# Feed-forward activations stored as two fp32r halves, with the loads, rows and norms of the down stages rearranged

## The chip, the cores and the metric

The kernel runs on one core of a Trainium2 chip. The metric is the device time of one execution in microseconds (us). The version before has a median of 2328.14 us over three runs (2327.58 to 2334.51). TensorE is called PE below, VectorE DVE, ScalarE ACT, GpSimd POOL, and the queue of SyncE, which issues nearly all transfers, SP.

## The reference, cut to what matters

Two layers run over 1024 tokens of width 1024. Each layer has a mixer and a feed-forward part, both inside sandwich RMSNorm (pre-norm, sub-layer, post-norm, residual add):

```python
def sandwich(x, g_pre, g_post, fn):
    return x + rmsnorm(fn(rmsnorm(x, g_pre)), g_post)

def swiglu(h, w_gate, w_up, w_down):
    return (jax.nn.silu(h @ w_gate) * (h @ w_up)) @ w_down
```

The change sits in the two `swiglu` parts. Their inner width is 2816, which is 22 blocks of 128.

## The kernel before, in words

**Split arithmetic.** A product of float32 matrices is made of three matmuls in fp32r: an operand `a` is kept as a high half `hi` (a rounding to fp32r) and a low half `a - hi`, and the products high-high, high-low and low-high are added (`mm3`, line 114; `hi`/`lo` are written `wh`/`wl` for weights, `hh`/`hl` for h). `wsplit` (line 1118) makes the halves of a weight tile: an ACT cast for `wh` (line 1121), a POOL subtraction for `wl` (line 1123).

**Up stage** (`Ffn.up`, line 1218; `pair`, line 1168). For 11 pairs of blocks, Strassen-like sums of weights and inputs give seven products per pair instead of eight, 24 matmuls each. From these come four quarters of h per pair (SiLU on ACT, line 1144, and a product on DVE, line 1145) and three sums of quarters on POOL (`store`, line 1178). All seven tiles of 128 x 512 go to DRAM as plain float32 (`h_s`, blocks 0 to 6, lines 1147 and 1179). In layer 0 the preparation of the state-space layer (`s5_prep`, line 578) runs as a generator beside the pairs: one step at each `emit` and each `store`. Its tiles tagged `pbig` have six buffers.

**Down stage** (`Ffn.down`, line 1229). For each group of two pairs, seven products with sums of `w_down` blocks accumulate into two SBUF tiles `out`. `hx` (line 1249) loads a block of h (512 KB for two pairs, four buffers, on SP) and splits it again: ACT makes `hh` (line 1252), DVE makes `hl` (line 1253). `drain` (line 1262) adds PSUM to `out`, mostly on DVE (line 1271). After the last `top`, the rows of the first half of `out` go through `end` while the last two products of the second half run; then the second half follows.

**Row norms** (`sandwich`, line 157). Per 128 tokens: the residual row is loaded into `r` (line 162), ACT sums the squares (line 106), POOL makes the reciprocal root (lines 97 and 98), DVE scales by it and by the post-norm gain (line 165) and adds the residual (line 166), the row is stored (line 170), and in layer 0 a second sum of squares and a second scaling (line 173) follow for the next layer. In layer 1 the two scalings are lines 168 and 169. In layer 0 the rows are then transposed on PE (`to_T`, line 175) as input of `mla_in` (line 807).

**Order.** The framework orders the instructions of each engine ahead of time by a simulated timeline; each engine, and SP, then runs its own list strictly in order. A load whose buffer is not free holds all that stand behind it in SP's list. The gains of the post-norm (`gpost`, `gpre`, line 111) and the rows `r` are loaded as early as that order places them, which is at the start of the down stage.

Of the kernel before, what the change touches and what calls it, by code (L numbers as in the profile page):

```python
# [10 lines left out]
F32 = mybir.dt.float32  # L11
# [24 lines left out]
class Trunk:  # L36
# [64 lines left out]
    def sumsq(self, a):  # L101
        ss = self.small.tile([P, 1], F32, tag="ss", name="ss")
        junk = self.tmp.tile([P, D], BF16, tag="t", name="junk")
        if len(a.shape) == 3:
            junk = junk.rearrange("p (k c) -> p k c", k=2)
# [3 lines left out]
    def bcast(self, pool, ap, name):  # L109
        t = pool.tile([P, D], F32, tag=name, name=name, bufs=1)  # L110
        self.nc.sync.dma_start(t, ap.partition_broadcast(P))
        return t
# [44 lines left out]
    def sandwich(self, acc, tb, res, hout, gpost, gpre, r, eng, m=None):  # L157
# [420 lines left out]
    def s5_prep(self, pool):  # L578
# [7 lines left out]
        big = lambda n: pool.tile([P, 2, 9 * 16], F32, tag="pbig", name=n, bufs=6)  # L586
# [58 lines left out]
        tb = sm("tb", (P, 8, 16))  # L645
# [18 lines left out]
        for ch in range(2):  # L664
# [28 lines left out]
            de = sm("de", (32, 4, 16))  # L693
# [360 lines left out]
class Ffn:  # L1054
    def __init__(self, K, p, left, right):
        self.K, self.nc, self.left, self.right = K, K.nc, left, right
        self.gu, self.dn = K.io[p + "gu"], K.io[p + "dn"]
        self.h_s = K.dr.tile([7, NF // 2, P, HALF], F32, name=p + "h_s")
# [82 lines left out]
    def emit(self, g, u, blk, i):  # L1141
# [4 lines left out]
        if blk is not None:  # L1146
            nc.sync.dma_start(self.h_s[blk, i], g)

    def pre(self, i, step):
# [8 lines left out]
        else:  # L1158
# [5 lines left out]
            self.emit(c[0], c[1], 0, i)  # L1164
# [3 lines left out]
    def pair(self, i):  # L1168
# [32 lines left out]
        self.emit(c12[:, 0], c12[:, 1], None, i)  # L1201
        store(c11[1], c11[0], c12[:, 0], ALU.subtract, 6)
# [330 lines left out]
```

## Time and profile before

| What | us |
|---|---|
| median of three runs | 2328.14 |
| the profiled execution | 2332.52 |
| its span | 2330.1 |
| mean granted TensorE clock of it | 0.968 |
| up stage of layer 0 / down stage of layer 0 (from the span's start) | about 538 to 961 / 961 to 1197 |
| up stage of layer 1 / down stage of layer 1 | about 1676 to 2081 / 2081 to 2330 |

The profiled execution is 4.4 us above the median of the runs, and 2.4 us of it lie outside the span. Times in the rows are counted from the span's start. PE's busy time is modelled, since matmuls overlap, so its waits say more than its busy share.

### The profile page before, as it was taken

The numbers are of one execution on the slowest core, as the hardware profiler recorded it, in microseconds if no ns is written. First come the engines' busy times: TensorE is split into PE (matmuls) and PEld (weight loads), VectorE is DVE, ScalarE is ACT, GpSimd is POOL, SyncE is SP. The second block draws the span as 40 slices with busy tenths as digits, with TensorE's granted clock in tenths as the row PEclk, the third lists the DMA queues.
The fourth block names the chain that finished last, engine by engine and source line by source line (L and its number), as shares of the span: only waits on it lengthen the run. The fifth ranks groups of instructions, "written<-read, shape, count | busy, mean of one in ns | idle before, by whom it ended". The sixth has DMA issues, their size and how long they took to land.

```text
span 2330.1 us, 27167 instructions
## 1 busy us (share of the span) xinstructions
PE 2157.9 (93%) x9684; PEld 1746.3 (75%) x9684; DVE 1594.9 (68%) x2175; ACT 945.2 (41%) x1413; POOL 1265.7 (54%) x740
## 2 busy tenths in 40 slices
PE   7999889898999999899969888999899999989987
PEld 5887677676788878687758767876688888878866
DVE  6859567689856865477884578656964444447788
ACT  5554555453222332333344346654532322234332
POOL 4997202134665556776644455421575656577674
PEclk9999999899999999899979999999999999999999
DMA  5234683243332343644542674324332323255354
GB/s 204 71 109 140 167 206 112 76 168 107 107 117 100 123 136 104 221 140 134 173 160 80 193 232 141 113 97 160 119 131 72 133 73 131 73 178 185 112 167 149
DMA packets 150662, 315.32 MB, mean 135 GB/s; under 512 B 20224, under 2 KB 43904, under 8 KB 150528
## 3 DMA queue, kind: packets, MB, share of 16 engines
q1 hardware_dynamic: 150528, 313.60, 41.4%
q8 instruction: 76, 1.25, 0.2%
q14 instruction: 58, 0.48, 0.1%
HBM read 214.39 MB, written 96.01 MB: 133 GB/s over the span
## 4 chain that ended last, share of the span: by engine, by line
PE 68%; DVE 16%; DMA 6%; issue 4%; ACT 3%; POOL 3%; SPq 0%; POOLq 0%; DVEq 0%; ACTq 0%
PE b L115 29%; PE psd L115 13%; PE psw L115 6%; PE psc L115 5%; PE psq L115 3%; PE po L115 2%; DVE hl L1253 2%; DVE acc L1271 2%; PE pss L1038 2%; PE trp L365 1%; POOL wl L1123 1%; DVE wt L1042 1%; PE pss L452 1%; DMA bm<-k_s 1%; PE psv L115 1%
## 5 line engine op out<-in xcount | busy, mean ns | idle before, releaser
L1123 POOL TENSOR_TENSOR wl<-raw,wh 128x1024 fp32r<-128x1024 f32 (+1 forms) x238 | 614.1, 2588 | 412.3 <-ACT wh L1121 399.7
L115 PE MATMUL b<-T,wh 128*128 128x512 f32 x1408 | 438.4, 392 | 2.2 <-DVE F L1172 2.2
L1121 ACT CAST wh<-raw 128x1024 fp32r<-128x1024 f32 (+1 forms) x238 | 241.9, 1023 | 433.0 <-PE b L115 251.7
L115 PE MATMUL b<-B,wh 128*128 128x512 f32 x1056 | 337.4, 400 | 15.0 <-DVE c L1163 10.5
L115 PEld LDWEIGHTS b<-T,wh 128*128 128x128 f32 x1408 | 263.8, 188 | 62.3 <-issue 2.8
L115 PE MATMUL b<-T,wl 128*128 128x512 f32 x704 | 276.4, 393 | 1.6 <-POOL wl L1123 1.6
L115 PE MATMUL psd<-wh,hh 128*128 128x512 f32 x616 | 240.6, 400 | 32.6 <-ACT hh L1252 18.9
L115 PEld LDWEIGHTS b<-B,wh 128*128 128x128 f32 x1056 | 203.0, 193 | 62.5 <-ACT B L1089 7.3
L115 PE MATMUL psd<-wl,hh 128*128 128x512 f32 x616 | 241.4, 396 | 0.0
L115 PE MATMUL psd<-wh,hl 128*128 128x512 f32 x616 | 235.2, 396 | 1.3 <-DVE hl L1253 1.3
L1271 DVE TENSOR_TENSOR acc<-acc,psd 128x512 f32<-128x512 f32 (+1 forms) x208 | 177.8, 884 | 60.1 <-PE psd L115 60.0
L115 PE MATMUL b<-B,wl 128*128 128x512 f32 x528 | 210.9, 400 | 3.6 <-POOL wl L1123 3.6
L115 PE MATMUL psw<-wh,jt 128*128 128x512 f32 x512 | 176.0, 410 | 16.0 <-ACT jt L488 9.3
L1172 DVE TENSOR_TENSOR p<-p,b 128x1024 f32<-128x1024 f32 (+1 forms) x88 | 83.5, 950 | 135.3 <-PE b L115 134.9
L1252 ACT CAST hh<-hr 128x1024 fp32r<-128x1024 f32 (+1 forms) x84 | 82.2, 979 | 223.8 <-PE psd L115 206.6
L115 PEld LDWEIGHTS psd<-wh,hh 128*128 128x128 f32 x616 | 117.2, 190 | 67.3 <-ACT hh L1252 23.9
L1253 DVE TENSOR_TENSOR hl<-hr,hh 128x1024 fp32r<-128x1024 f32 (+1 forms) x84 | 152.5, 1826 | 16.6 <-ACT hh L1252 16.6
L115 PEld LDWEIGHTS b<-T,wl 128*128 128x128 f32 x704 | 132.1, 188 | 32.7 <-POOL wl L1123 2.8
L91 POOL TENSOR_TENSOR wl<-raw,wh 128x1024 fp32r<-128x1024 f32 x48 | 122.2, 2558 | 58.4 <-ACT wh L89 58.4
L115 PEld LDWEIGHTS psd<-wh,hl 128*128 128x128 f32 x616 | 117.1, 190 | 28.9 <-DVE hl L1253 2.6
L115 PEld LDWEIGHTS psd<-wl,hh 128*128 128x128 f32 x616 | 117.5, 191 | 25.5
L1173 DVE TENSOR_TENSOR raw<-raw 128x1024 f32<-128x1024 f32 x66 | 106.7, 1617 | 41.3 <-POOL wl L1123 40.2
(386 smaller groups left out, 4314.4 us busy)
## 6 DMA issues: line engine op xcount, KB each, us to landing
raw<-in_l_gu_dram SPq DMA_DIRECT2D x96, 512.0 KB, 3.6
hr<-l_h_s SPq DMA_DIRECT2D x70, 512.0 KB, 4.1
raw<-in_l_dn_dram SPq DMA_DIRECT2D x48, 512.0 KB, 3.8
l_h_s<-F SPq DMA_DIRECT2D x66, 256.0 KB, 2.3
raw<-in_w_in_dram SPq DMA_DIRECT2D x27, 512.0 KB, 3.5
l_h_s<-c SPq DMA_DIRECT2D x44, 256.0 KB, 2.1
l_h_s<-p SPq DMA_DIRECT2D x44, 256.0 KB, 2.6
raw<-in_l_w_out_dram SPq DMA_DIRECT2D x16, 512.0 KB, 4.2
```

The costliest lines, as they stand in the source:

```text
L91: nc.gpsimd.tensor_tensor(lo, raw, hi.bitcast(F32), op=ALU.subtract)
L115: mm = lambda *t, **k: self.nc.tensor.matmul(*t, skip_group_check=go, **k)
L365: nc.tensor.transpose(tr[:, jj * P:(jj + 1) * P], Wt[:, offs[jj] + i * P:offs[jj] + (i + 1) * P], self.ident)
L452: nc.tensor.matmul(ps[:, b0:b0 + bw], Q[c][v][:, j * P:(j + 1) * P], M[c][:, b0:b0 + bw], start=v == 0, stop=v == 1)
L1038: nc.tensor.matmul(ps[:, ks], a[:, js], b[:, ks], start=first, stop=last)
L1121: nc.scalar.copy(hi[:, 0:n], r[:, 0:n])
L1123: nc.gpsimd.tensor_tensor(lo[:, 0:n], r[:, 0:n], hi[:, 0:n].bitcast(F32), op=ALU.subtract)
L1172: add = lambda o, a, b: v.tensor_tensor(o, a, b, op=ALU.add)
L1173: sub = lambda o, a, b: v.tensor_tensor(o, a, b, op=ALU.subtract)
L1252: nc.scalar.copy(hi[:, 0:n], r[:, 0:n])
L1253: v.tensor_tensor(lo[:, 0:n], r[:, 0:n], hi[:, 0:n].bitcast(F32), op=ALU.subtract)
L1271: v.tensor_tensor(dst, dst, ps, op=ALU.add)
```

## The change

1. **Halves in DRAM.** `h_s` gets a further dimension of two. A new method `put` makes the halves in the up stage: ACT copies the tile into `hs` (fp32r, two buffers), SP stores that, the low half is subtracted in place, on POOL for the blocks 6, 1, 5 and 4 (the sums that POOL itself made) and on DVE for 3, 0 and 2, and SP stores it too. `hx` then loads both halves (1 MB for two pairs, four buffers) and splits nothing.
2. **First loads.** The loads of the blocks 0, 5, 1 and 4 of the first group are issued by ACT.
3. **Late rows and gains.** The gains and the first four residual rows get a small ACT copy from `out` first, so that their loads cannot start before the last but one `top` has been added up. The eight rows are loaded there and passed to `end`.
4. **Staggered norms.** `sandwich` becomes a generator `sand` with pauses; `skew` runs the rows of one half shifted by one stage against each other. All four rows of the first half go before the last two products. In layer 0 the second half's sums of squares wait for the last transposed piece of the first half.
5. **Room.** `pbig` in `s5_prep` has three buffers instead of six, and three small tiles move into other tags. In layer 1 the two extra buffers of the split weights are closed during the up stage (`K.less()`, `K.more(right)`), so `wh` and `wl` have three buffers there instead of five.

```diff
-        self.h_s = K.dr.tile([7, NF // 2, P, HALF], F32, name=p + "h_s")
+        self.h_s = K.dr.tile([7, NF // 2, P, 2, HALF], F32, name=p + "h_s")
...
+    def put(self, blk, i, g):
+        nc = self.nc
+        hi = self.hs.tile([P, HALF], F32R, tag="hs", name="hs", bufs=2)
+        nc.scalar.copy(hi, g)
+        nc.sync.dma_start(self.h_s[blk, i, :, 0], hi.bitcast(F32))
+        eng = nc.gpsimd if blk in (6, 1, 5, 4) else nc.vector
+        eng.tensor_tensor(g.bitcast(F32R), g, hi.bitcast(F32), op=ALU.subtract)
+        nc.sync.dma_start(self.h_s[blk, i, :, 1], g)
...
-        both(u4, 3)
-        store(c12[:, 1], c12[:, 0], u4[:, 0], ALU.add, 1)
-        store(u4[:, 1], c12[:, 1], c11[0], ALU.subtract, 5)
+        both(u4)
+        pool(c12[:, 1], c12[:, 0], u4[:, 0], ALU.add)
+        self.put(3, i, u4[:, 0])
+        pool(u4[:, 1], c12[:, 1], c11[0], ALU.subtract)
+        self.put(0, i, c11[0])
+        self.put(1, i, c12[:, 1])
...
-        both(p1, 2)
-        store(p1[:, 1], p1[:, 0], u4[:, 1], ALU.subtract, 4)
+        both(p1)
+        pool(p1[:, 1], p1[:, 0], u4[:, 1], ALU.subtract)
+        self.put(5, i, u4[:, 1])
+        self.put(2, i, p1[:, 0])
+        self.put(4, i, p1[:, 1])
...
-        def hx(blk, i, n):
-            r = hraw(blk, i, n)
-            hi, lo = half("hh"), half("hl")
-            nc.scalar.copy(hi[:, 0:n], r[:, 0:n])
-            v.tensor_tensor(lo[:, 0:n], r[:, 0:n], hi[:, 0:n].bitcast(F32), op=ALU.subtract)
-            return hi, lo
+        def hx(blk, i, n):
+            r = hp.tile([P, 2, 2, HALF], F32R, tag="h", name="h", bufs=4)
+            queue = nc.scalar if i == 0 and blk in (0, 5, 1, 4) else nc.sync
+            queue.dma_start(r[:, 0:n].bitcast(F32), self.h_s[blk, i:i + n].rearrange("g p s c -> p g s c"))
+            return r
...
         top(i1, n)
+        late = out[0][:, 0, 0, 0:1]
+        gains(late)
+        rows = []
+        for tb in range(8):
+            r = ap.tile([P, D], F32, tag="r", name="r", bufs=4)
+            if tb < 4:
+                nc.scalar.copy(r[:, 0:1], late)
+            nc.sync.dma_start(r, res[tb * P:(tb + 1) * P, :])
+            rows.append(r)
         B = top(i2, n)
...
-        end(0, out[0], rows(2), 0)
+        end(0, out[0], rows[0:4], 0)
...
-        end(0, out[0], rows(2), 2)
...
+    def skew(self, rows):
+        live = []
+        for g in [*rows, None, None]:
+            for x in [g] * (g is not None) + live[::-1]:
+                next(x, None)
+            live.append(g if g is not None else iter(()))
...
-        big = lambda n: pool.tile([P, 2, 9 * 16], F32, tag="pbig", name=n, bufs=6)
+        big = lambda n: pool.tile([P, 2, 9 * 16], F32, tag="pbig", name=n, bufs=3)
...
+    K.less()
     G.up()
+    K.more(right)
```

## Rows read from the trace of the kernel before

**Rows 1.** The page: the chain that ended last, by engine.
```profile
PE 68%; DVE 16%; DMA 6%; issue 4%; ACT 3%; POOL 3%; SPq 0%; POOLq 0%; DVEq 0%; ACTq 0%
```

**Rows 2.** Busy time by stretch: start:end, us, engines (instructions), clock, DMA share, GB/s.
```profile
975.00:1100.00 125.00, 125.00 (x540) 102.12 (x539) 90.35 (x86) 46.67 (x54) 81.84 (x35) 0.99 0.45 148
...
1680.00:2080.00 400.00, 400.00 (x1739) 326.70 (x1739) 197.29 (x201) 113.07 (x125) 244.08 (x117) 1.00 0.30 102
```

**Rows 3.** PE's first down matmul of layer 0 in the timeline, idle time before it.
```profile
972.51 0.80 PE L115 MATMUL psd<-wh,hh 128*128 128x512 f32 x1 [11.61 <-ACT hh L1252]
```

**Rows 4.** The chain of waits, 905 to 985 us: start, us, what.
```profile
956.36 6.06 DMA gpost<-in_l_ffn_post_dram
...
962.44 8.95 DMA hr<-l_h_s
...
972.51 12.69 PE psd L115 x43
```

**Rows 5.** Transfers: up stage of layer 1, then 975 to 1100 us; us to landing.
```profile
l_h_s<-F SPq DMA_DIRECT2D x30, 256.0 KB, 2.5
...
hr<-l_h_s SPq DMA_DIRECT2D x18, 512.0 KB, 3.8
```

**Rows 6.** Who waited for whom on PE, 2079 to 2092 us: us, times, longest.
```profile
PE psd L115 <- ACT hh L1252: 5.4, 1, 5.4
PE psd L115 <- DVE hl L1253: 1.3, 1, 1.3
```

**Rows 7.** Busy time by stretch around the ends of the up and down stages.
```profile
964.30:978.00 13.70, 5.49 (x13) 4.02 (x14) 5.30 (x4) 5.22 (x5) 9.01 (x5) 0.50 1.04 405
2083.80:2094.00 10.20, 6.29 (x14) 4.51 (x15) 7.59 (x3) 3.14 (x3) 8.08 (x4) 0.50 0.92 333
...
1196.00:1210.00 14.00, 1.29 (x9) 0.93 (x8) 9.41 (x9) 6.13 (x11) 7.86 (x10) 0.63 0.55 181
1210.00:1222.00 12.00, 6.56 (x25) 4.51 (x23) 10.53 (x11) 5.19 (x10) 3.48 (x5) 0.50 0.50 172
```

**Rows 8.** Who waited for whom on PE, 1100 to 1197 us, then 2215 to 2319 us.
```profile
PE psd L115 <- DVE acc L1271: 4.2, 6, 1.5
...
PE psd L115 <- DVE acc L1271: 9.3, 7, 2.4
```

**Rows 9.** A group on DVE, 1100 to 1200 us: busy, mean ns, idle before.
```profile
L1253 DVE TENSOR_TENSOR hl<-hr,hh 128x1024 fp32r<-128x1024 f32 x14 | 26.6, 1900 | 0.0
```

**Rows 10.** Timeline of DVE: the first scaling of three rows.
```profile
1177.66 1.29 DVE L165 SCALAR_TENSOR_TENSOR acc<-acc,rstd,gpost 128x1024 f32<-128x1024 f32 x1 [1.00 <-ACT hh L1252]
...
1188.15 3.41 DVE L165 SCALAR_TENSOR_TENSOR acc<-acc,rstd,gpost 128x1024 f32<-128x1024 f32 x1 [0.72 <-ACT wh L89]
...
1199.24 3.36 DVE L165 SCALAR_TENSOR_TENSOR acc<-acc,rstd,gpost 128x1024 f32<-128x1024 f32 x1
```

**Rows 11.** Timeline of SP in the up stage of layer 0.
```profile
815.86 11.31 SPq L699 DMA_DIRECT2D T_s<-K  x16
...
942.19 14.08 SPq L1115 DMA_DIRECT2D raw<-in_l_dn_dram  x3
```

**Rows 12.** The chain of waits, 2290 to 2331 us: the last row.
```profile
2325.09 1.28 DVE r L169
```

**Rows 13.** Groups on POOL, ACT and DVE in layer 1's up stage, 1680 to 2080 us.
```profile
L1123 POOL TENSOR_TENSOR wl<-raw,wh 128x1024 fp32r<-128x1024 f32 x72 | 181.3, 2519 | 142.7 <-ACT wh L1121 133.3 <-DMA raw<-in_l_gu_dram 9.3
L1178 POOL TENSOR_TENSOR F<-F 128x512 f32<-128x512 f32 x11 | 14.3, 1297 | 13.6 <-DVE F L1145 13.6
...
L1121 ACT CAST wh<-raw 128x1024 fp32r<-128x1024 f32 x72 | 75.7, 1052 | 212.2 <-PE b L115 143.2 <-DVE raw L1173 51.2 <-POOL wl L1123 9.1
L1144 ACT ACTIVATE F<-F 128x512 f32<-128x512 f32 x22 | 13.9, 632 | 51.5 <-DVE F L1172 51.5
...
L1145 DVE TENSOR_TENSOR F<-F 128x512 f32<-128x512 f32 x22 | 17.2, 783 | 2.0
```

**Rows 14.** Who waited for whom on PE, 538 to 960 us.
```profile
PE b L115 <- POOL wl L1123: 5.2, 4, 3.5
```

More of the change, by code (lines that the diff above doesn't have):

```diff
@@ L99, in rstd, with sumsq @@
         return r
-    def sumsq(self, a):
+    def sumsq(self, a, late=None):
         ss = self.small.tile([P, 1], F32, tag="ss", name="ss")
         junk = self.tmp.tile([P, D], BF16, tag="t", name="junk")
+        if late is not None:
+            self.nc.scalar.copy(junk[:, 0:1], late)
         if len(a.shape) == 3:
@@ L107, in sumsq, with bcast @@
         return self.rstd(ss, D, RMS_EPS)
-    def bcast(self, pool, ap, name):
+    def bcast(self, pool, ap, name, late=None):
         t = pool.tile([P, D], F32, tag=name, name=name, bufs=1)
+        if late is not None:
+            self.nc.scalar.copy(t[:, 0:1], late)
         self.nc.sync.dma_start(t, ap.partition_broadcast(P))
@@ L161, in sandwich @@
         acc, r = v3(acc), v3(r)
-        nc.sync.dma_start(r, v3(res[rows, :]))
-        rs = self.sumsq(acc)
+        if res is not None:
+            nc.sync.dma_start(r, v3(res[rows, :]))
+        rs = self.sumsq(acc, late)
         if m is None:
             nc.vector.scalar_tensor_tensor(acc, acc, rs, v3(gpost), op0=ALU.mult, op1=ALU.mult)
+            yield
             eng.tensor_tensor(r, r, acc, op=ALU.add)
@@ L172, in sandwich @@
             rs = self.sumsq(r)
+            yield
             nc.vector.scalar_tensor_tensor(acc, r, rs, v3(gpre), op0=ALU.mult, op1=ALU.mult)
@@ L1200, in pair @@
         c11 = self.c11.pop(i)
-        self.emit(c12[:, 0], c12[:, 1], None, i)
-        store(c11[1], c11[0], c12[:, 0], ALU.subtract, 6)
+        both(c12)
+        pool(c11[1], c11[0], c12[:, 0], ALU.subtract)
+        self.put(6, i, c11[1])
         sub(A21, A11, A21)
@@ L1227, in up, with down @@
         self.xs.close()
-    def down(self, end, ap):
+    def down(self, end, ap, gains, res):
         nc, K, v = self.nc, self.K, self.nc.vector
@@ L1235, in down @@
         seen = set()
-        half = lambda tag: hp.tile([P, 2, HALF], F32R, tag=tag, name=tag, bufs=4)
         def ld(blk, i, n):
@@ L1320, in down @@
         W4 = [w4(B, n, v)]
-        rows = lambda k: [ap.tile([P, D], F32, tag="r", name="r", bufs=4) for _ in range(k)]
-        end(0, out[0], rows(2), 0)
+        end(0, out[0], rows[0:4], 0)
         C12, C22 = ld(1, i1, n), ld(3, i1, n)
@@ L1334, in down @@
         hs.close()
-        end(1, out[1], rows(4), 0)
+        end(1, out[1], rows[4:8], 0)
 @with_exitstack
```

48 lines of the change are left out of this document (22 added, 26 removed).

## The prediction

> **What bounds the kernel now.** I read the chain that ended last first, by engine [rows 1]: two thirds of the span are PE, so the question in each stage is whether PE waits there at all. The table of stretches answers it [rows 2]: in the up stage of layer 1 and in the middle of the down stage of layer 0 PE is busy from end to end (1739 matmuls in 400 us, 0.230 us each, so 5.5 us per product of 24). Work taken off other engines there is worth nothing. PE waits at the edges of the down stages, in three kinds of places.
>
> *Starts.* In layer 0 PE stands still for 11.61 us before the first down matmul [rows 3]. The chain [rows 4] shows why: SP issues the gains at 956.36, the first h load only at 962.44, and the load takes 8.95 us, against a median of 3.8 in the middle of the stage [rows 5], because gains and four residual rows are in flight ahead of it. In layer 1 PE waits 5.4 and 1.3 us for the two halves of the first h [rows 6]. After both gaps the granted clock is 0.50 (the 1.2 GHz level): PE was busy 5.49 and 6.29 us in those stretches [rows 7], and at 2.4 GHz this would have taken half, so 2.7 and 3.1 us go with the gaps.
>
> *Last groups.* PE waits 4.2 us in layer 0 and 9.3 us in layer 1 for DVE to empty PSUM [rows 8]. DVE is late because the low halves of h stand in its list: 14 of 1.900 us, with no idle time before them [rows 9].
>
> *The change of layers.* The last down matmul of layer 0 ends near 1197 and the projections begin near 1222. In between PE is busy 1.29 and 6.56 us out of 26 [rows 7]. It waits for the row norms, which run one after another: the first scalings of three rows start at 1177.66, 1188.15 and 1199.24, 10.8 us apart [rows 10], although the wait-free scalings take 1.29 us and a row has three DVE passes, so about 3.9 us.
>
> **The change, part by part.** The sum is made against the profiled execution, 2332.5 us, which lies 4.4 above the median of the runs.
>
> *Start of layer 0.* The ACT queue does not hold behind SP's weight loads (three of which kept SP 14.08 us here [rows 11]), gains and rows come later, and no split follows the load. At stake: 11.6 + 2.7 = 14.3 us. I cannot see where ACT's list will put the load; if right behind the last SiLU, near 959, a load of twice 512 KB at 4 to 5 us (above the 3.8 of one [rows 5]) lands 3 to 4 us after PE is free. I take 10 saved; bounds 3 and 14.3.
>
> *Start of layer 1.* At stake 5.4 + 1.3 + 3.1 = 9.8 us. The split goes for certain, the load's own time may stay: 6 saved; bounds 2 and 9.8.
>
> *Last groups.* Without the 26.6 us of low halves DVE has room for the drains in the 100 us of that stretch. Of 4.2 and 9.3 us I take 4 and 8; bounds 0 and all.
>
> *The change of layers.* Staggered, the rows cost DVE some 3.9 us each instead of 10.8. Four rows are 16 us, and beside them run 22 us of matmuls (the last two products of two groups, 96 matmuls at 0.230), with eight drains. So the first half is normed about when PE finishes, and its transposes need some more us. I let 9 of the 25 us stay and take 16; bounds 5 and 20. The weights of the projections are made by POOL meanwhile, which covers them unless PE comes much earlier than this.
>
> *The end.* The last scaling starts at 2325.09 [rows 12], behind a chain row by row after the last matmul near 2318; staggering shortens it a little: 2; bounds 0 and 4.
>
> *The puts.* Each pair gets seven ACT copies of 512 columns, nearest row 0.632 us (the SiLU of the same tile) [rows 13], 4.4 us; four POOL subtractions at 1.297, 5.2 us; three DVE subtractions at 0.783, 2.3 us; and seven more stores. POOL then carries 7 x 2.52 + 8 x 1.30 = 28 us of a pair's 37, ACT under 16, DVE some 20. None fills the pair, and what hides them is that weights are made ahead: with three buffers a `wh` may start when PE frees one, two products or 11 us before its use, and cast and subtraction take 1.05 + 2.52, so an order that runs up to 7.5 us late costs nothing. What queues behind a put is the next `wh` on ACT: `hs` has two buffers, puts come in threes (3, 0, 1 and 5, 2, 4), and the third copy waits for the first one's store, 2.5 us to landing [rows 5]. In layer 1 I take 2 us for the stage; bounds 0 and 10. In layer 0 SP also issues the 16 pieces of `T_s` in 11.31 us [rows 11], twice. A store of halves behind them holds `hs`, then ACT, then `wl` for longer than 7.5 us. With three `pbig` buffers, DVE's next step of `s5_prep` waits besides for PE's transposes and for a store. PE already waits 5.2 us on `wl` in this stage [rows 14]. I take 6; bounds 0 and 18.
>
> *The middle of the down stages.* The loads double. The stretch moves 148 GB/s at a DMA share of 0.45 [rows 2]; with about 11.5 MB more in 125 us it would be 240 GB/s, at a share near 0.7. The queue can carry it (405 GB/s at a share of 1.04 [rows 7]), but a buffer is now held until PE is done with it, four products deep, and SP waits in order with weight loads behind. Four products are 22 us against a load of some 5, so most is hidden: 4 us for both layers; bounds 0 and 24.
>
> *ACT's six tiny copies* per layer wait for a drain. They come when that drain is due, and what queues behind them is a `wh` with 7.5 us in hand: nothing.
>
> The sum: 10 + 6 + 12 + 16 + 2 = 46 saved, 2 + 6 + 4 = 12 paid, so 34 less: 2298.5 for an execution like the profiled one, **2294** at the median.
>
> **The rivals.**
>
> *The up stages take half of it back.* Third copies and `T_s` stores hold ACT beyond the 7.5 us in some pairs: 18 in layer 0 and 10 in layer 1 instead of 8, with the middle of the down stages at 10 instead of 4. That is 26 more: 2320. For it: two buffers, and PE's waits on `wl` already there. Against it: the up stage of layer 1 shows PE without a gap.
>
> *The first loads stay late.* They carry twice the bytes, and no wait of SP need be what mattered. Then 16 us of the starts are not saved: 2310. For it: 8.95 us of the start are the load itself [rows 4]. The Trainium skill (DMA: Bandwidth & Descriptors, section "Issuing engines are not separate DMA queues") says that transfers from several engines run on the same 16 DMA engines and that another issuer only saves issue time. By that rule the start gains what SP's wait cost and no transfer time. The rows ahead speak partly against it: 8.95 against 3.8 us is traffic that the change itself moves away.
>
> *Slower: ACT becomes the limit of the up stages.* If in every pair the hi store stands behind a waiting weight load in SP's list, the third copy holds ACT, `wh` comes late, and each pair loses what exceeds the 7.5 us. Over 22 pairs it takes 1.9 us per pair (41 us: the 34 gained and 7 more) to be slower than before. A store held like the loads in [rows 11], 14.08 us, in one place of each pair would lose about 4 us after the 2.5 it needs anyway: 88 us, in place of the 8 charged, 2374. Against it: PE's waits on `wl` total 5.2 us over eleven pairs today, with three buffers.
>
> *The change does not do what it says at the edges*: the order puts the late rows or the norms no earlier, and only the drains gain: about 2316.
>
> **How the numbers follow.** About 0.3% (7 us) is what a measurement of this kernel can tell from no change. The forecast has 0.60, the half given back 0.15, late first loads 0.09, no earlier norms 0.05, slower 0.11. The forecast's own range, with its bounds, is 2276 (upper ends of the gains, little paid) to 2312. Faster by over 0.3% are the forecast, the late loads, the norms and about half of the case that gives half back: 0.82. Within 0.3% are 0.07, slower 0.11. The range to 2320 leaves out the slower case and some of the half given back.
>
> **What would show it.** Right: PE's wait before the first down matmul under 5 us in both layers, no DVE low halves of h, at most 10 us between the last down matmul of layer 0 and the projections, first scalings about 4 us apart, and up stages of the same length within 5 us. Wrong: PE waits on `wl` of more than 10 us in an up stage, with ACT idle on a store of `hs`; or waits on h loads in the middle of a down stage.

## The result, and the profile after

The changed kernel takes 2345.52 us (2345.06 to 2350.44, four runs) against 2328.16 for the kernel before: a ratio of 1.007, interval 1.005 to 1.009. It is slower by 0.7%; 2294 was predicted, 1.5% faster. The profiled span grew from 2330.1 to 2348.7 us.

To see where, I cut both spans at the starts of PE's own marks: the first product on a sum (`T`) and the last matmul of each up stage, the first and last down matmul (`psd`), the first projection (`psu`). A gap thus holds the last up matmul too and is 0.4 us longer than PE's wait.

| Stretch, us | before | after | difference | predicted |
|---|---|---|---|---|
| up to the first `T` product of layer 0 | 546.7 | 552.1 | +5.4 | 0 |
| up stage of layer 0, from there | 413.8 | 445.6 | **+31.8** | +6 |
| gap before the first down matmul, layer 0 | 12.0 | 8.8 | −3.2 | −10 with the clock |
| down stage of layer 0 | 222.4 | 221.0 | −1.4 | −4, and +2 for its middle |
| change of layers | 25.3 | 15.1 | −10.2 | −16 |
| mixer of layer 1 | 463.3 | 460.6 | −2.7 | 0 |
| up stage of layer 1 | 397.1 | 399.5 | +2.4 | +2 |
| gap before the first down matmul, layer 1 | 5.8 | 9.5 | **+3.7** | −6 with the clock |
| down stage of layer 1 | 231.3 | 226.6 | −4.7 | −8, and +2 for its middle |
| end | 12.4 | 9.9 | −2.5 | −2 |

The differences sum to +18.6. Among the versions below the first row lies between 545.7 and 554.2 and the mixer's between 453.5 and 467.1, so nothing is read from these two.

**Up stage of layer 0.** Stretches of the changed kernel, in the columns of [rows 2]; the last row is the up stage of layer 1:

```profile
565.00:640.00 75.00, 61.33 (x250) 47.96 (x249) 69.62 (x104) 24.43 (x33) 52.66 (x27) 0.95 0.40 142
640.00:740.00 100.00, 100.00 (x442) 82.38 (x441) 74.37 (x63) 36.46 (x48) 76.62 (x38) 1.00 0.40 141
740.00:905.00 165.00, 147.62 (x626) 115.89 (x626) 143.80 (x160) 56.85 (x83) 104.59 (x54) 0.96 0.44 149
...
1700.00:2100.00 400.00, 397.80 (x1731) 325.67 (x1730) 282.37 (x229) 149.32 (x192) 316.86 (x153) 1.00 0.41 146
```

The loss is not spread over the pairs. In the second stretch PE is busy 100.00 of 100 us, and from 905 to 990 us it is busy throughout, although every pair has its seven puts; in the other two it is idle 13.7 and 17.4 us. The same two stretches before, 5.4 us earlier:

```profile
559.60:634.60 75.00, 68.76 (x284) 54.38 (x283) 66.37 (x143) 18.60 (x24) 45.40 (x21) 0.95 0.33 107
...
734.60:899.60 165.00, 163.91 (x730) 133.26 (x731) 120.45 (x150) 48.55 (x64) 93.88 (x46) 1.00 0.37 123
```

There PE was idle 6.2 and 1.1 us, so the change adds 7.4 and 16.3 us of idle time. The other 8 us of the 31.8 are PE's own work: it is busy 414.90 us in the whole stage after and 406.88 before (rows under g4 below), with the granted clock at 0.98 in place of 0.99. In both stretches DVE (third busy column) runs `s5_prep` beside the pairs and is busy 69.62 of 75 and 143.80 of 165 us, where it was busy 66.37 and 120.45 before. In the quiet stretches it is at 72 to 74%. The sums of the inputs, which f1's expectation below names for the first stretch, end at 559.6 us; what DVE carries there are the first steps of `s5_prep`. Two of them, lines 655 and 659, with the POOL instruction beside the second, from the timeline of all engines, 570 to 584 us:

```profile
571.92 0.15 DVE L655 TENSOR_TENSOR k<-ai,lam 128x8 f32<-128x8 f32 x1
...
580.77 2.40 POOL L1142 TENSOR_TENSOR wl<-raw,wh 128x1024 fp32r<-128x1024 f32 x1 [3.62 <-ACT wh L1140]
580.83 2.38 DVE L659 TENSOR_TENSOR k<-nr,lam 128x8 f32<-128x8 f32 x1
```

An instruction on eight columns takes 0.15 us, and 2.38 when it begins just after a `wl` of POOL.

Who waited for whom from 550 to 998 us (total, times, longest):

```profile
POOL wl L1142 <- ACT wh L1140: 70.6, 25, 10.6
...
ACT hs L1169 <- POOL c L1204: 52.4, 10, 7.8
...
ACT hs L1169 <- DVE c L1172: 22.1, 7, 3.5
...
PE b L119 <- POOL wl L1142: 15.2, 10, 3.2
ACT hs L1169 <- DVE F L1172: 13.5, 4, 7.0
...
ACT hs L1169 <- DMA l_h_s<-hs: 11.1, 10, 4.4
...
PE b L119 <- ACT wh L1140: 8.2, 3, 3.9
```

PE's wait on `wl` is 15.2 us where [rows 14] had 5.2, and 8.2 us on `wh` are new. ACT's copies `hs` wait 52.4 us for their input, the sum that POOL makes. Their waits for line 1172, the subtraction, are waits for a buffer: `hs` has two, and a copy can start only when the subtraction that reads the copy before the last one is done (22.1 us for that of block 0, 13.5 for that of block 3). Only 11.1 us are waits for a store. And this is how POOL and DVE meet, from the timeline of all engines, 616 to 630 us:

```profile
621.84 0.70 DVE L1172 TENSOR_TENSOR F<-F,hs 128x512 fp32r<-128x512 f32 x1 [0.82 <-POOL F L1204]
621.89 1.80 POOL L1204 TENSOR_TENSOR F<-F,c 128x512 f32<-128x512 f32 x1
...
623.65 2.79 POOL L1142 TENSOR_TENSOR wl<-raw,wh 128x1024 fp32r<-128x1024 f32 x1
...
624.16 2.83 DVE L1172 TENSOR_TENSOR c<-c,hs 128x512 fp32r<-128x512 f32 x1
...
626.49 0.50 PE L119 MATMUL b<-T,wl 128*128 128x512 f32 x1 [2.09 <-POOL wl L1142]
```

A DVE subtraction of one shape takes 0.70 us, and 2.83 when a `wl` of POOL began just before it. All subtractions (line 1172) of the up stage of layer 0, then of layer 1, with the busy time of DVE and of POOL:

```profile
552.10:998.10 446.00, 39.49 (x30) 68.63 (x41) 0.98 0.41 143
...
1703.10:2103.00 399.90, 48.87 (x30) 75.61 (x41) 1.00 0.42 148
```

Subtractions that I priced at 1.297 us on POOL and 0.783 on DVE by [rows 13] took 1.67 and 1.32 on average in layer 0, and 1.84 and 1.63 in layer 1, where the stage lost 2.4 us. So the price alone does not make the loss.

**Starts.** ACT's timeline, 995 to 1008 us, then the load in layer 1 (2100 to 2116):

```profile
997.75 0.62 ACT L1163 ACTIVATE p<-p 128x512 f32<-128x512 f32 x1
1000.61 0.62 ACT L1169 CAST hs<-F 128x512 fp32r<-128x512 f32 x1 [2.25 <-DVE F L1164]
1000.70 0.91 ACTq L1278 DMA_DIRECT2D h<-l_h_s  x2
...
2106.38 0.37 ACTq L1278 DMA_DIRECT2D h<-l_h_s  x1
```

PE's first down matmul in layer 1, from its timeline, answers [rows 3]:

```profile
2112.16 0.76 PE L119 MATMUL psd<-wh,h 128*128 128x512 f32 x1 [9.12 <-DMA h<-l_h_s]
```

PE's waits from 2096 to 2145 us answer [rows 6]:

```profile
PE psd L119 <- DMA h<-l_h_s: 17.3, 2, 9.1
```

The last up matmul of layer 0 starts at 997.7. A copy of the last pair stands in ACT's list ahead of the load and waits for DVE's product, so the load goes out 3.0 us later; the first of the four lands 5.6 us after its issue. In layer 1 these are 3.7 and 5.6 us, where before the load went out 0.6 us ahead of that matmul and landed 5.3 us later. There the fifth load, the first that SP issues, costs PE another 8.2 us: in SP's list it stands behind the last pair's stores and goes out at 2121.13. The clock falls as before, in the columns of [rows 7]:

```profile
1000.00:1010.20 10.20, 3.72 (x9) 2.98 (x10) 6.76 (x5) 3.11 (x5) 10.04 (x6) 0.52 0.82 296
...
2106.00:2116.20 10.20, 4.04 (x10) 3.21 (x11) 7.78 (x5) 2.70 (x4) 10.20 (x5) 0.52 0.83 306
2123.00:2133.20 10.20, 5.07 (x12) 4.04 (x13) 1.68 (x2) 2.51 (x3) 5.45 (x4) 0.52 0.81 301
```

The third row follows that second wait, so layer 1 now has two such stretches instead of one.

**Last groups and the change of layers.** PE's waits on the drains, 1132 to 1228 us and 2236 to 2339 us ([rows 8]), and on the transposes from 1227 to 1262:

```profile
PE psd L119 <- DVE acc L1296: 2.6, 3, 1.3
...
PE psd L119 <- DVE acc L1296: 0.5, 2, 0.3
...
PE tr L200 <- DVE xt L203: 7.5, 3, 6.4
```

No group of DVE makes low halves of h there any more ([rows 9]). The first scalings of four rows ([rows 10]) come in pairs:

```profile
1202.79 1.28 DVE L181 SCALAR_TENSOR_TENSOR acc<-acc,rstd,gpost 128x1024 f32<-128x1024 f32 x1
...
1204.79 3.41 DVE L181 SCALAR_TENSOR_TENSOR acc<-acc,rstd,gpost 128x1024 f32<-128x1024 f32 x1
...
1215.80 1.29 DVE L181 SCALAR_TENSOR_TENSOR acc<-acc,rstd,gpost 128x1024 f32<-128x1024 f32 x1 [0.72 <-POOL rstd L98]
...
1220.74 3.43 DVE L181 SCALAR_TENSOR_TENSOR acc<-acc,rstd,gpost 128x1024 f32<-128x1024 f32 x1
```

Four rows span 18 us, where three spanned 21.6 (the fourth of before starts at 1209.36).

### The profile page after: what moved, and what is told of

The parts are those of the page before. It is cut to its first block, busy times and chain, and to the rows that moved or that the text cites. A ratio compares the mean times of both kernels' runs of the same rounds, so it can differ in the third digit from the quotient of the medians.

```text
span 2348.7 us, 27676 instructions
## 1 busy us (share of the span) xinstructions
PE 2162.6 (92%) x9684; PEld 1751.3 (75%) x9684; DVE 1640.4 (70%) x2157; ACT 956.4 (41%) x1498; POOL 1395.7 (59%) x828
## 5 line engine op out<-in xcount | busy, mean ns | idle before, releaser
L1142 POOL TENSOR_TENSOR wl<-raw,wh 128x1024 fp32r<-128x1024 f32 (+1 forms) x238 | 583.7, 2459 | 286.4 <-ACT wh L1140 271.1
L119 PE MATMUL psd<-wh,h 128*128 128x512 f32 x1232 | 391.3, 397 | 31.4 <-DMA h<-l_h_s 25.7
L119 PEld LDWEIGHTS psd<-wh,h 128*128 128x128 f32 x1232 | 234.3, 190 | 89.6 <-issue 26.9
L119 PE MATMUL b<-T,wl 128*128 128x512 f32 x704 | 279.9, 398 | 14.7 <-POOL wl L1142 14.5
L1296 DVE TENSOR_TENSOR acc<-acc,psd 128x1024 f32<-128x1024 f32 (+1 forms) x208 | 181.7, 890 | 156.1 <-PE psd L119 155.8
L119 PE MATMUL psd<-wl,h 128*128 128x512 f32 x616 | 243.7, 396 | 0.0
L119 PEld LDWEIGHTS psd<-wl,h 128*128 128x128 f32 x616 | 117.4, 191 | 25.8
L119 PEld LDWEIGHTS psw<-wh,jt 128*128 128x128 f32 x512 | 97.0, 193 | 44.5 <-ACT jt L507 17.5
L231 POOL TENSOR_TENSOR yconv<-yconv,cm 128x512 f32<-128x512 f32 x90 | 120.8, 1346 | 6.4 <-ACT cm L230 1.2
L97 POOL TENSOR_SCALAR rstd<-ss 128x1 f32<-128x1 f32 x64 | 36.4, 569 | 143.0 <-ACT junk L108 138.0
L119 PEld LDWEIGHTS b<-B,wl 128*128 128x128 f32 x528 | 101.5, 192 | 26.0 <-POOL wl L1142 4.3
```

The costliest lines, as they stand in the source:

```text
L97: nc.gpsimd.tensor_scalar(r, ss, 1.0 / n, eps, op0=ALU.mult, op1=ALU.add)
L119: mm = lambda *t, **k: self.nc.tensor.matmul(*t, skip_group_check=go, **k)
L231: nc.gpsimd.tensor_tensor(y, y, m, op=ALU.add)
L1142: nc.gpsimd.tensor_tensor(lo[:, 0:n], r[:, 0:n], hi[:, 0:n].bitcast(F32), op=ALU.subtract)
L1296: v.tensor_tensor(dst, dst, ps, op=ALU.add)
```

## The experiments

Stage lengths, from each run's profiled execution, by the marks above:

| Version | up 0 | gap 0 | change | up 1 | gap 1 | down 1 | end | median, ratio to before |
|---|---|---|---|---|---|---|---|---|
| before | 413.8 | 12.0 | 25.3 | 397.1 | 5.8 | 231.3 | 12.4 | |
| after | 445.6 | 8.8 | 15.1 | 399.5 | 9.5 | 226.6 | 9.9 | 2345.52, 1.007 |
| e1 norms alone | 416.6 | 5.3 | 20.1 | 397.2 | 5.8 | 231.2 | 12.7 | 2318.99, 0.9954 |
| e2 norms and room | 412.9 | 7.0 | 20.2 | 396.4 | 4.5 | 230.7 | 12.3 | 2319.01, 0.9947 |
| e3 halves in layer 1 | 416.0 | 5.5 | 20.1 | 399.7 | 9.3 | 226.1 | 9.8 | 2316.1, 0.994 |
| e4 first loads on SP | 447.5 | 11.5 | 15.1 | 397.5 | 11.4 | 223.7 | 9.9 | 2350.31, 1.0086 |
| f1 pairs 0, 1 plain | 434.3 | 25.8 | 11.6 | 399.0 | 8.7 | 225.5 | 9.8 | 2345.8, 1.0059 |
| f2 quiet pairs plain | 445.4 | 3.5 | 19.1 | 399.1 | 9.4 | 225.3 | 9.9 | 2346.78, 1.0072 |
| f3 third buffer | 448.3 | 9.6 | 14.7 | 400.1 | 9.5 | 228.7 | 9.8 | 2348.15, 1.0071 |
| f4 copies on POOL | 446.6 | 5.4 | 14.7 | 398.3 | 6.6 | 225.4 | 9.9 | 2346.55, 1.0061 |
| g1 stores alone | 421.3 | 3.5 | 15.2 | 396.2 | 6.6 | 216.2 | 9.9 | 2299.34, 0.987 |
| g2 no subtractions | 417.3 | 5.9 | 15.2 | 395.1 | 6.8 | 224.0 | 9.9 | 2306.13, 0.9899 |
| g3 low halves on DVE | 432.3 | 9.1 | 14.7 | 398.9 | 9.3 | 225.6 | 9.9 | 2336.64, 1.0029 |
| g4 low halves on POOL | 451.1 | 10.3 | 14.7 | 403.1 | 10.2 | 225.8 | 9.9 | 2356.09, 1.0113 |
| h1 first load alone | 447.8 | 9.7 | 15.1 | 399.1 | 9.5 | 227.9 | 9.9 | 2349.82, 1.0087 |
| h2 last pairs, a | 411.1 | 24.7 | 18.7 | 396.1 | 11.5 | 222.9 | 9.9 | 2325.99, 0.999 |
| h3 last pairs, b | 422.4 | 24.6 | 14.7 | 395.2 | 11.5 | 223.1 | 10.1 | 2329.05, 0.9999 |
| h4 no stagger | 412.3 | 7.0 | 25.2 | 395.2 | 4.2 | 229.7 | 13.3 | 2325.29, 0.9988 |
| k1 last sums on DVE, last pairs | 413.2 | 21.4 | 19.2 | 396.1 | 13.0 | 222.5 | 9.9 | 2326.75, 0.9985 |
| k2 last sums on DVE, halves | 447.3 | 8.9 | 14.7 | 397.7 | 9.6 | 225.2 | 9.9 | 2341.74, 1.0054 |

The six versions that store nearly all of layer 0 plainly (before, e1, e2, e3, h2, k1) and h4 have an up 0 of 411.1 to 416.6, so a difference under some 5 us there says little. The down stage of layer 0, which has no column, lies between 218 and 226 us, but at 232 in f4, where PE waits 11.6 us once for a drain on ACT.

### Parts alone: e1, e2, e3, e4

e1 stores h plainly in both layers and keeps the late rows and the staggered norms; e2 keeps the part "room" as well:

```diff
     def put(self, blk, i, g):
+        if not self.halves:
+            nc.sync.dma_start(self.h_s[blk, i], g)
+            return
...
-        big = lambda n: pool.tile([P, 2, 9 * 16], F32, tag="pbig", name=n, bufs=3)
+        big = lambda n: pool.tile([P, 2, 9 * 16], F32, tag="pbig", name=n, bufs=6)
...
-    K.less()
     G.up()
-    K.more(right)
```

(`pbig` and `less` change in e1 alone.) e3 has halves in layer 1 and `pbig` at six. e4 is the changed kernel with

```diff
-            queue = nc.scalar if i == 0 and blk in (0, 5, 1, 4) else nc.sync
+            queue = nc.sync
```

> Left out of the change: the halves in DRAM (h is stored and split as before), the room edits (six pbig buffers, five weight buffers in layer 1) and with them ACT's first loads. Kept: late rows and gains, staggered norms. Both theories of the lost 32 us of layer 0's up stage (puts, or room) expect that stage back at about 414 us from its first to its last T product (after: 446). Norms: the gap between the last down matmul of layer 0 and the projections 12 to 15 us, as after, not 25. The waits on DVE in the last groups come back, 4 and 9 us. Time 2300 to 2312. If the late gains do not matter for the start of the down stage of layer 0, its 11.6 us stay and the time is at the upper end; if they do, 5 to 8 us are left.

> As the run before, but with the room edits: three pbig buffers, tb, de and it in other tags, and three weight buffers in layer 1's up stage. Theory room (DVE and ACT steps of s5_prep wait on each other because their buffers are three): layer 0's up stage 435 to 446 us, time 20 to 30 us above the run before. Rival puts (the hs copies hold ACT's list): the up stage stays at 414 to 420, time within 6 us of the run before.

> Halves in layer 1 alone; layer 0 stores and splits h as before and keeps six pbig buffers. Theory (layer 1's gain of the halves in the last groups, about 9 us of waits and the slow stretch with them, is given back at the start of its down stage, 17 us of waits on h loads against 7): time within 5 us of e1. Rival (halves pay where no s5_prep runs beside): 8 to 15 us below e1.

> The change with the first h loads on SP instead of ACT, nothing else. Theory ACT's list (the loads stand behind a copy that waits 8 to 9 us for POOL): on SP they are issued earlier, PE's waits on h at the two starts, 8.4 and 17.3 us, shrink by 5 us or more together. Rival bytes (4 MB of first loads and the stores of the last pair fill the DMA engines): waits the same within 3 us each. Third possibility: SP's list is held by stores that wait for POOL, and the waits grow. Time 2338 to 2352.

Measured: without halves the kernel is faster than before, 0.9954 (0.9938 to 0.9971) and 0.9947 (0.9927 to 0.9966), and up 0 has its old length with three `pbig` buffers and three weight buffers too. So the loss comes from the halves in layer 0, and "room" alone costs nothing: that theory fell (six `pbig` buffers beside the halves of layer 0 were not tried). e3 has the lowest ratio of the versions that do the whole computation, 0.994 (0.9921 to 0.9959), though not clear of e1 and e2; its halves shorten down 1 and the end by about 5 and 3 us and lengthen gap 1 and up 1 by about 4 and 3. With the first loads on SP the gaps are 11.5 and 11.4: ACT's queue saves some 2 to 3 us.

### Where in the stage: f1, f2

f1 stores the pairs 0 and 1 of layer 0 plainly, f2 the pairs 2, 3, 9 and 10:

```diff
+        if i not in self.halved:
+            nc.sync.dma_start(self.h_s[blk, i, :, 0], g)
+            return
```

> Layer 0 stores the pairs 0 and 1 plainly (and splits them again in the down stage's first group); all other pairs as halves. Up stage of layer 0 with halves 445.6 us, without 412.9. Theory 'copies meet a late DVE' (PE's gaps lie only where DVE is full: 568 to 632 us, beside the sums of the inputs, and 752 to 897, beside the state-space preparation): the early gaps, some 14 us, go nearly all, the later ones stay; up stage about 432. Rival 'every put costs the same': 2 of 11 pairs, so 6 us of 32 go, and what goes is spread: about 440.

> Layer 0 stores the pairs 2, 3, 9 and 10 plainly, whose puts lie where PE shows no gap in the changed kernel. Theory 'copies meet a late DVE': up stage of layer 0 stays within 4 us of 445.6. Rival 'every put costs the same': 4 of 11 pairs, so 12 us go: about 434.

f1's up 0 is 434.3, f2's 445.4: two pairs bring 11 us, four others nothing. Two stretches of f1, in the same columns, which answer to the first and the third one above:

```profile
559.00:634.00 75.00, 70.27 (x298) 56.35 (x297) 64.53 (x109) 18.87 (x22) 42.56 (x21) 0.98 0.30 100
...
734.00:889.00 155.00, 137.18 (x581) 107.24 (x582) 135.94 (x154) 52.40 (x76) 96.35 (x51) 0.97 0.44 147
```

PE's idle time in the first stretch falls from 13.7 to 4.7 us, in the later one it is 17.8. The place decides, not the number of puts. h2 and h3 below agree: with halves for the pairs 7 and 8 as well, made while `s5_prep` runs, h3's up 0 is 11.3 us longer. f1 gains no time as a whole: its plain loads of the first group wait in SP's list, and gap 0 grows to 25.8.

### What in a put costs the time: f3, f4, g1 to g4

```diff
-        self.put(1, i, c12[:, 1])
+        self.put(1, i, c12[:, 1], c12[:, 0].bitcast(F32R))
```

is f3 (the third argument takes the place of `hs`, for block 1 alone); f4, g2, g3 and g4 change `put`:

```diff
+        if blk in (6, 1, 5, 4):
+            nc.gpsimd.tensor_copy(hi, g)
+        else:
+            nc.scalar.copy(hi, g)
...
-        eng.tensor_tensor(g.bitcast(F32R), g, hi.bitcast(F32), op=ALU.subtract)
...
-        eng = nc.gpsimd if blk in (6, 1, 5, 4) else nc.vector
+        eng = nc.vector
...
+        eng = nc.gpsimd
```

in this order. g1 leaves the copy out too and stores the plain tile twice.

> The high half of block 1 goes into a tile that is free by then, so no copy of three in a row waits for a store. My prediction's step (the third copy waits for the first one's store and holds ACT): up stage of layer 0 gains 15 us or more, to 430 or less. Theory 'the copy waits for its input, not for its buffer' (52.4 us of ACT's waits for POOL's sums and 35.6 for DVE's against 11.1 for its stores): 0 to 5 us, 441 to 446.

> The high halves of the blocks 6, 1, 5 and 4 are made by POOL, which made these sums itself, so ACT's list never waits for POOL's sums. Theory 'the copy that waits for its input holds the casts of weights behind it': the up stage of layer 0 gains 10 to 20 us (to 426 to 436) although POOL gets 44 copies more. Rival 'POOL and DVE are too full, the copies only show it': POOL, 315 us busy of 446, gets about 50 us more; the up stage stays or grows, 446 to 460.

> Both layers store the plain tile twice, in place of a high and a low half: no copy on ACT, no subtraction (this leaves the splitting of h out). So the doubled traffic of the up stages stands alone. Theory 'late DVE': the up stage of layer 0 goes back from 445.6 to 412 to 418 us. Rival 'the stores themselves, 14 per pair in SP's list in front of the weight loads': 430 us or more.

> ACT makes the high halves as in the changed kernel, but nothing is subtracted: the plain tile is stored as the low half (this leaves the low halves out). Theory 'the subtractions load DVE and POOL, and DVE becomes late': 412 to 422 us in the up stage of layer 0. Rival 'the copies in ACT's list hold the casts behind them, whatever DVE carries': 435 or more.

> All seven subtractions of a pair on DVE. Theory 'late DVE': DVE carries 44 more, some 1.3 to 1.9 us each as the 20 of the changed kernel, so the up stage of layer 0 grows to 452 to 475 us. Rival 'POOL is the one that is late' (its 71 weight halves at 2.5 us and 44 subtractions): POOL loses 44, and the stage falls to 425 to 438.

> All seven subtractions of a pair on POOL. Theory 'late DVE': DVE loses 33 subtractions (some 45 us busy), and the up stage of layer 0 falls to 425 to 438 us. Rival 'POOL is late': 33 more on POOL at 1.3 us, 315 us busy becoming some 360 of 446: 450 to 465. If DVE's other instructions only grow slower beside more POOL work, it stays within 6 us of 445.6.

f3: 448.3. Among its waits from 550 to 1003 us ACT's wait for its stores is 4.5 us instead of 11.1, and nothing was gained. Against its expectation the second three (5, 2, 4) still shares two buffers, and the waits for subtractions that read a buffer stay (17.1 us for that of block 0), so f3 tests the stores and not the buffers:

```profile
POOL wl L1142 <- ACT wh L1140: 98.4, 31, 10.5
...
ACT hs L1170 <- DMA l_h_s<-hs: 4.5, 4, 1.6
```

f4: 446.6, although POOL's late sums hold ACT no more; POOL has 44 copies more. Among the waits of f4 from 550 to 995 us, PE now waits on `wh`:

```profile
PE b L119 <- ACT wh L1140: 13.1, 6, 6.1
```

g1 and g2: 421.3 and 417.3. Doubled stores, in g2 with 77 copies, cost 4 to 8 us; the subtractions cost the other 24 to 28. This in spite of 14 stores per pair, and of copies that wait longer for their stores than in the changed kernel. So neither the copies nor the stores make the loss. Among the waits of g2 from 550 to 968 us:

```profile
POOL wl L1142 <- ACT wh L1140: 149.1, 52, 10.6
...
ACT hs L1169 <- DMA l_h_s<-hs: 43.6, 19, 9.4
```

g3 and g4 turn against the theory as I had put it. With all subtractions on DVE, which was to make a late DVE later, the stage falls to 432.3; with all on POOL it grows to 451.1. The rival, that POOL is late, gave both (425 to 438 and 450 to 465). But the third case of g4's expectation, that DVE's other instructions only grow slower beside more work of POOL, holds too: 451.1 is 5.5 above 445.6. The whole stage of before, after, g2, g3 and g4, in the columns of [rows 2], shows that this happens:

```profile
546.70:960.90 414.20, 406.88 (x1777) 329.66 (x1775) 288.80 (x399) 119.42 (x144) 250.72 (x118) 0.99 0.33 109
...
552.10:998.10 446.00, 414.90 (x1778) 333.04 (x1776) 364.51 (x420) 156.27 (x213) 315.42 (x157) 0.98 0.41 143
...
550.50:968.20 417.70, 406.14 (x1778) 329.04 (x1777) 293.94 (x390) 157.93 (x215) 241.99 (x117) 1.00 0.45 153
...
551.00:983.60 432.60, 413.18 (x1778) 331.75 (x1776) 366.28 (x461) 154.73 (x211) 248.16 (x115) 0.98 0.43 147
...
549.90:1001.40 451.50, 418.17 (x1778) 333.39 (x1777) 347.23 (x389) 152.70 (x211) 346.38 (x186) 0.97 0.41 140
```

In g4 DVE makes no subtraction and is still busy 347.23 us, 53 more than in g2, where nobody makes one. The 71 subtractions of POOL that fall into the stage lengthen DVE's other instructions by that much, 0.75 us each. In g3 DVE makes the 71 itself, in 84 us, and its other instructions take 282 us, less than in g2. In the changed kernel these others take 325 us (364.51 less 39.49). So a subtraction given to POOL is not taken off DVE: it costs both engines time.

POOL's wait for `wh` is its slack. Slack of 149.1 (g2), 130.2 (g3, below) and 70.6 us (after) goes with a stage of 417, 432 and 446, but f3 has 98.4 at 448.3, so it does not order the versions, and a late list of POOL is not shown as the cause. The waits of g3:

```profile
POOL wl L1142 <- ACT wh L1140: 130.2, 44, 10.5
```

What the runs show is this: the subtractions cost 24 to 28 us, beside `s5_prep`; with all of them on DVE the stage is 13 us shorter than with the change's division, with all on POOL 5 us longer. Between g2 and g3 POOL's busy time hardly differs (241.99 and 248.16 us), and 15 us come with 77 subtractions on DVE. How the rest divides between POOL's own lateness and DVE's slowing beside POOL is not shown.

### The starts: h1, k1, k2, with h2 and h3

h1 sends only block 0 of the first group over ACT:

```diff
-            queue = nc.scalar if i == 0 and blk in (0, 5, 1, 4) else nc.sync
+            queue = nc.scalar if i == 0 and blk == 0 else nc.sync
```

h2 has halves only for the pairs 9 and 10 in layer 0 and 7 to 10 in layer 1 (by the lines of f1) with `eng = nc.vector`, h3 for 7 to 10 in both. k1 is h2, k2 the changed kernel, each with

```diff
-            self.nc.gpsimd.tensor_tensor(o, x, y, op=op)
+            (v if i == NF // 2 - 1 else self.nc.gpsimd).tensor_tensor(o, x, y, op=op)
```

and in k2 the last pair's subtractions on DVE. POOL makes four sums per pair (blocks 6, 1, 5 and 4), not three.

> Of the first group's loads of h only block 0 is issued by ACT; 5, 1 and 4 go back to SP. Theory 'four loads of 1 MB in flight together share the transfers, so the first lands as late as the fourth': PE's gap before the first down matmul falls from 8.8 and 9.5 us to 6 or less in both layers, the second wait (8.6 us in layer 1) may grow. Rival 'ACT's list is held before it issues the loads': the gaps stay within 1.5 us.

> Halves only for the pairs 9 and 10 in layer 0 and 7 to 10 in layer 1, all low halves on DVE; the other pairs are stored plainly and split in the down stage. Theory 'loss only where DVE and POOL are full': up stages as without halves (413 to 416 and 396 to 399), the start of layer 1 as without halves (about 5 us), the tail of layer 1 at 9.8 instead of 12.7, the change of layers 15 instead of 20, the down stage of layer 1 near 226: about 2306 to 2311. Rival 'what halves give at the change of layers needs them in all groups': 2314 to 2319.

> The same with halves for the pairs 7 to 10 in layer 0 also. These pairs 7 and 8 are made while DVE carries the state-space preparation. Theory 'loss only where DVE and POOL are full': up stage of layer 0 about 420 (8 us more than without halves), the change of layers 15: 2309 to 2316. If the loss were spread over the pairs, 4 of 11 of the 19 us that halves with all subtractions on DVE cost: 420 as well, so this run is for the time; the page shows where the gaps lie.

> As last_pairs_a, with the three sums of the last pair on DVE in both layers. Theory 'POOL's late sum holds ACT, and with it the last stores and the first loads': the gaps at the starts fall from 24.7 and 11.5 us to 5 to 9 in layer 0 and 4 to 7 in layer 1: about 2302 to 2309. Rival 'the stores of halves at the end of the stage stand in SP's list before the loads anyway': the gaps fall by less than 5 us: 2318 to 2326.

> The changed kernel with the three sums and all subtractions of the last pair on DVE. Theory 'POOL's late sum holds ACT': gaps of 8.8 and 9.5 us fall to 4 to 6 in both layers (as in copies_on_pool, 5.4 and 6.6), the up stages keep their length: about 2338 to 2342. Rival 'the first loads of 1 MB need their time': the gaps stay within 1.5 us.

h1: the gaps stay, 9.7 and 9.5, although ACT issues only one load (5.8 us to landing); SP issues the next 1.5 us later, so the first is nearly alone for that time only. That four loads share the transfers is not shown to be the reason. k2: POOL's late sum is gone from ACT's list, and the gaps stay too, 8.9 and 9.6: the theory of that hold fell, and the gaps stayed within 1.5 us, as "the first loads of 1 MB need their time" had it. ACT's timeline of k2, 975 to 1010 us:

```profile
997.65 0.62 ACT L1169 CAST hs<-F 128x512 fp32r<-128x512 f32 x1 [1.75 <-DVE F L1164]
997.74 0.91 ACTq L1278 DMA_DIRECT2D h<-l_h_s  x2
```

Its last up matmul starts at 994.5: 3.2 us to the issue, 5.6 to the landing. The hold of 8 us lay before that matmul and cost nothing there. f4 and g1, whose loads go out about when the last matmul of layer 0 starts and 1.6 us before, have gaps of 5.4 and 3.5, with 5.4 and 4.9 us to the first landing of the same 1 MB. So what sets these gaps apart is when the load goes out: in the changed kernel and k2 it stands behind the last pair's copy, which waits for DVE.

h2, h3 and k1 were meant to beat both kernels and did not: 0.999 (0.9976 to 1.0004), 0.9999 (0.9983 to 1.0014) and 0.9985 (0.997 to 1.0). Their up stages are as short as hoped, their ends too, but the plain first loads come late. SP's timeline of k1, 935 to 990 us:

```profile
935.16 20.07 SPq L1135 DMA_DIRECT2D raw<-in_l_dn_dram  x3
...
973.76 2.74 SPq L1283 DMA_DIRECT2D hr<-l_h_s  x4
```

The last up matmul starts at 959.8. Between these two rows stand the last pair's stores of halves, each behind an ACT copy and a subtraction, and the loads wait behind them in SP's list. Halves for the last pair and plain loads for the first group, both on SP, do not go together. The same with the plain first loads on ACT was not tried.

### The staggering: h4

h4 is e2 with the rows of each half one after another:

```diff
     def skew(self, rows):
+        for g in rows:
+            for _ in g:
+                pass
+        return
```

> As norms_and_room (no halves; late rows and gains), but the rows of each half run one after another in program order instead of staggered. My prediction put the gain at the change of layers down to the staggering: it goes back from 20.2 to about 25 us and the tail stays. If the order planned ahead staggers them anyway, it stays at 20. The start of layer 0 keeps its gain (7.0 against 12.0 us before), if the late rows and gains made it.

The change of layers goes from 20.2 back to 25.2 us, and the median to 0.9988 (0.9976 to 0.9999). Scalings of h4:

```profile
1169.88 1.28 DVE L185 SCALAR_TENSOR_TENSOR acc<-acc,rstd,gpost 128x1024 f32<-128x1024 f32 x1 [0.99 <-ACT hh L1290]
...
1180.37 3.41 DVE L185 SCALAR_TENSOR_TENSOR acc<-acc,rstd,gpost 128x1024 f32<-128x1024 f32 x1 [0.72 <-ACT wh L89]
...
1191.47 3.36 DVE L185 SCALAR_TENSOR_TENSOR acc<-acc,rstd,gpost 128x1024 f32<-128x1024 f32 x1
```

They are 10.5 and 11.1 us apart, as in [rows 10]: the staggering is worth 5 us. Gap 0 stays at 7.0, so the staggering did not make that gain, and late rows and gains are what is left.

## Why the prediction was wrong, step by step

The forecast was 34 less, the spans show 18.6 more, 52.6 apart. Half of it is one term.

**The puts in layer 0: 6 (0 to 18) predicted, 31.8 measured.** This is the step that failed, in three places. *The prices:* 1.297 us for POOL and 0.783 for DVE were rows of layer 1; the product of 0.783 already took 1.376 us in layer 0's up stage before the change, and the subtractions took 1.67 and 1.32. *The addition:* I summed busy time per engine over a mean pair, again by layer 1 ("DVE some 20", "none fills the pair"). In layer 0 DVE was busy 288.80 us before, about 26 for each of eleven pairs, and 66.37 of 75 us in one stretch, since `s5_prep` stands in its list. The change adds 39 us of its own subtractions and some 36 us by which DVE's other instructions grow longer, a term that I put at nothing. The gaps lie in the two stretches where `s5_prep` takes DVE to 93 and 87%, and a mean over eleven pairs hides both. *The holder:* I named the third copy's buffer and the stores of `T_s`. A copy does wait for a buffer, but 11.1 us for a store and 35.6 for a subtraction on DVE that still reads it; with 43.6 us of waits for stores g2 loses next to nothing, and stores alone cost 8 us at most (g1). My margin of 7.5 us for a `wh` left POOL's own queue out: behind a put on POOL queue not only a `wl` of 2.5 us but the sum before it and its wait for DVE. Taking 44 subtractions off POOL and giving them to DVE brings 13.3 us back (g3), putting 33 on it costs 5.5 more (g4). How the loss divides between DVE's own subtractions, its slowing beside POOL, and POOL's lateness is open.

**The puts in layer 1: 2 predicted, 2.4 measured.** Right in size, with the same wrong prices: DVE is at 282 of 400 us there without `s5_prep`. That this room absorbs them was not tested by itself.

**The middle of the down stages: 4 paid predicted, nothing measured.** From 1030 to 1140 us PE is busy all but 0.1 us, without a wait for h, at 225 GB/s and a DMA share of 0.66. I had 240 and 0.7, with 11.5 MB where the 18 loads of [rows 5] are 9.4:

```profile
1030.00:1140.00 110.00, 109.89 (x479) 89.24 (x478) 54.75 (x63) 22.02 (x24) 77.46 (x38) 1.00 0.66 225
```

**Start of layer 0: 10 saved predicted, 3.2 measured; layer 1: 6 saved predicted, 3.7 and a second wait of 8.2 lost.** Late rows and gains worked: gap 0 is 5.3 and 7.0 us in e1 and e2, and the first load lands in 4.2 us instead of 8.95. But with halves the load is 1 MB instead of 512 KB and its first landing takes 5.6 us where I took 4 to 5; and "right behind the last SiLU" was wrong: a copy of the last pair stands ahead, waiting for DVE, 3 us. The sum, 3.0 + 5.6 = 8.6, is nearly all of the gap of 8.8. In layer 1 the late rows bring little (gap 1 is 5.8 and 4.5 in e1 and e2). The load lands in 5.6 us there where 512 KB took 5.3 before, so the gap grew because the load goes out 4.3 us later against the last up matmul, and hardly by its bytes. The rival *the first loads stay late* had the size of this; of its reasons the bytes are the smaller part.

By the Trainium skill (DMA: Bandwidth & Descriptors, section "Issuing engines are not separate DMA queues") another issuer saves only issue time. The traces agree: in e4 the load goes out 5.1 us after the last up matmul of layer 0 starts instead of 3.0 and lands in 6.3 instead of 5.6, so the other queue saved issue time, 2.1 us, and hardly any of the transfer.

**Last groups: 4 and 8 saved.** PE's waits on the drains fell from 4.2 to 2.6 and from 9.3 to 0.5. Right in layer 1, where the second wait for h takes part of it back in the stage's length (4.7 us shorter); in layer 0 1.6 of 4, and what keeps the 2.6 was not tried.

**Change of layers: 16 saved predicted, 10.2 measured.** The mechanism was right, the size not: staggering brings 5 us (h4), the halves another 5 (20.2 to 15.1). I had counted 3.9 us per row; two of the four scalings shown take 3.4 us instead of 1.29, and four rows span 18 us. PE still waits 7.5 us for transposes.

**The end: 2 predicted, 2.5 measured,** and the halves, not the staggering, made it: it stays at 12.7 and 12.3 in e1 and e2.

**The rivals.** *Slower* was right in sign, at 0.11, and wrong in engine and place: I let ACT lose 4 us in every pair, for 2374; it is the subtractions on POOL and DVE, in the two stretches where `s5_prep` fills DVE. Of my signs of being wrong PE's wait on `wl` over 10 us came, but not with ACT idle on a store. I had seen that layer 0 runs `s5_prep`, and looked only at its stores.

## What to carry to other kernels

Moving work from one stage into another must be priced in the worst stretch of that stage, not on its mean, and with durations from there: DVE stood at 88 and 73% in the two stretches of layer 0 before the change, and at 49% in layer 1, where the same puts cost 2.4 us. Where two engines slow each other, work given to one has to be counted on the other as well (here 0.75 us of DVE for each subtraction on POOL). How long the in-order helper waits for its next input did not tell the versions apart. And an edge needs its own account: halves pay at the end of a down stage and cost at its start, here mostly because the first load goes out later, behind work of the last pair.

## What the runs showed of the hardware that was not expected

A DVE subtraction of 128x512 took 0.70 and 2.83 us within three microseconds, the longer one begun 0.5 us after a POOL subtraction of 2.79 us had started. Over the stage this is no small matter: subtractions that stand on POOL alone (g4) make DVE busy 53 us longer than none (g2).

By the Trainium skill (SBUF — State Buffer, section "Who interferes with whom") a DVE instruction with two SBUF inputs contends with a GpSimd instruction that reads SBUF, and the order of issue decides which of them blocks. These rows agree: the DVE subtraction begun inside POOL's 2.79 us ends 0.55 us after it, about the 0.70 that the work itself takes, and POOL's sum begun 0.05 us after the DVE subtraction of 0.70 us takes 1.80 us, where another of its shape at 620.50 took 1.30. Here that is 2.1 us more on DVE for one meeting. Moving 33 such subtractions from DVE to POOL does not avoid it: both up stages were longer, 451.1 and 403.1 us.
